# Attention scores and decay sums: the narrow products of one layer are given all 128 rows of the array

## The chip, the core and the metric

The kernel runs on one core of a Trainium2 chip. The metric is the device time of one execution in microseconds (us). A core has a tensor engine (PE) with an array of 128 rows by 128 columns, a vector engine (DVE), a scalar engine (ACT), a GpSimd engine (POOL), a queue engine for transfers (SP), an on-chip memory of 128 partitions and an accumulator memory (PSUM) that the PE writes. For every product the PE first loads a stationary operand (the profile lists that as PEld), then streams the columns of the other operand past it. How many partitions the operands have is how many rows of the array the product uses.

## The reference

One layer on 512 tokens of width 1024: an RMS norm, one projection into three token mixers (gated linear attention, softmax attention, gated DeltaNet), a gated merge of the three, an output projection, then a SwiGLU feed-forward and a last norm. The change touches two small places. In the softmax attention there are 8 heads of 64 channels, and each needs its scores:

```
qh = heads(q) * ATT_HD ** -0.5
scores = jnp.einsum('bhid,bhjd->bhij', q_, k_, preferred_element_type=F32) + bias
p = jax.nn.softmax(jnp.where(valid, scores, -jnp.inf), axis=-1)
```

In the DeltaNet the running sum of a head's log decays is needed along the columns of a score matrix:

```
gc = jnp.cumsum(to_chunks(log_alpha, GDN_HEADS)[..., 0], axis=-1)
gamma = jnp.exp(jnp.where(incl, gc[..., :, None] - gc[..., None, :], -jnp.inf))
```

## The kernel before

Operands are float32, but the large products run on a faster rounded form of it: each operand is split into a high part (rounded) and a low part (what is left), and a product is the sum of high x high, high x low and low x high. `mm3` (L162 to L165) issues these three. A projection (`proj_T`, tile `pj`) is 24 such products of 128 columns by 512 tokens; the value projection (`pv`), the merge (`br`) and the feed-forward (`ff`, `acc`) are of the same kind. They fill the PE from the start to the end.

Between them stand the small steps of the mixers. They are written as generators ("chains"), and `adv` traces as many of their steps behind each large product as a table of estimated delays (`LAT`) says are due. The result is one fixed order of instructions for each engine. An engine executes its own order strictly, and waits where an operand or a buffer is not ready.

**Attention.** `att_proj` prepares a pair of heads; a head has 64 channels, half of the partitions. For head 0 the query tile holds the high parts in partitions 0 to 63 and the low parts in 64 to 127; the key tile `k` has the high parts of the keys on both halves. So one product of 128 rows, L798, gives high x high plus low x high. The third term, query high x key low, is the second product, L799; the low parts of the keys of both heads share one tile `kl`, one head on each half, and the product takes 64 rows:

```
ps = SM("sc")
T.matmul(ps[:, 0:n_], q[hh][:, cs(qb)], k[hh][:, 0:n_], start=True, stop=False)
T.matmul(ps[:, 0:n_], q[hh][rows, cs(qb)], kl[rows, 0:n_], start=False, stop=True)
```

There are 4 pairs, 2 heads in each and 4 blocks of 128 queries, so 32 score tiles `sc`, with 256 to 512 columns. Behind them DVE scales and adds the bias (L801), takes the maximum (L804), ACT the exponential (L805), DVE the reciprocal and the scaling (L806, L807); the PE transposes the result (L813, `pT`), ACT copies it (L815), and the PE multiplies by the values (L822, `ov`; these products use 64 columns of the array).

**Decay sums.** `gcs` holds the high parts of the cumulated decays of the heads in partitions 0 to 7 and the low parts in 32 to 39, zeros between. A product with a selecting matrix `sel` (ones in two rows for a head) adds both and spreads the sum over 128 partitions (tile `rb`, 512 columns, 40 rows). It is done once per head in `gdn_k` (L578) and once in `gdn_q` (L616): 8 products.

Buffers come from pools in rotation. `U` tiles (29 buffers of 128 x 512) serve the queries, keys, convolved DeltaNet inputs (`cvo`) and others. Tiles `w`, `wh`, `wl` are the raw, high and low parts of a weight group (L151 on ACT, L155 on DVE).

Of the kernel before, what the change touches and what calls it, by code (L numbers as in the profile page):

```python
# [7 lines left out]
F32 = mybir.dt.float32  # L8
# [8 lines left out]
P = 128  # L17
S = 512
D = 1024
# [9 lines left out]
HP = 10000  # L29
# order of the projections between the chains  # L30
SEQ = "qyAzv01cdDsLa3rb2"
# [5 lines left out]
XE = "GAVVAAVV"  # L37
# start: 0-3 statistics of a token tile, a-d its norm and transposition, A-D its parts, w x the parts of a
# weight group, m n (M N) its products with the first (second) half of the tokens; engines of the halves of
# the token tiles (XE norm, LE low parts) and of the statistics (SQE), of the weights' parts (WHG, WLG)  # L40
START = "0w1abA2B3xmdcDCnMN"
NWARM = 14
SQE = "VVAV"
LE = "GVGVVVGG"
# estimated delays of the chains' steps, for the order in which they are traced
LAT = dict(ho0=9.069, ho1=0.144, ho2=0.738, ks0=0.985, ks1=0.887, ks2=1.018, gk0=1.523, gk1=3.393, gk2=18.451,
# [9 lines left out]
def trunk(ctx, tc, a, out, dbg=None):  # L56
# [26 lines left out]
    def U(s, dt=F32):  # L83
        return up.tile([P, 512], dt, tag="u", name=nm(s))
# [20 lines left out]
    def h4(t):  # L105
        return t.rearrange("p (h n) -> p h n", n=128)
# [11 lines left out]

# [1 line left out]
    cst = cp.tile([P, 8 * P], F32, name="cst")  # L120
# [25 lines left out]

# [1 line left out]
    def parts(raw, n=1024, eng=None, hi_eng=None):  # L148
# [18 lines left out]
    def preload(after):  # L167
        """The table set with both Exp and Ln, right behind `after`."""
        with tc.high_priority():
            p = A.preload_act_table_set(LNEXP)  # L170
        if after is not None:
            tc.add_manual_dep(p.ins, after.ins.name,
                              mybir.DependencyInfo(mybir.DependencyClass.NoSync, mybir.DependencyReason.DATA),
                              reason="act tables")
# [7 lines left out]
    def rsqrt(y, v):  # L182
        """y = v ** -0.5, one Newton step behind the tables."""
        t = st.tile([P, 16], F32, tag="nw", name=nm("nw"), bufs=4)[:, 0:y.shape[1]]
        A.activation(t, v, AF.Ln)
        A.activation(y, t, AF.Exp, scale=-0.5)
        newton(y, v, t)

# [1 line left out]
    def sq_sum(x, dst, eng=None):  # L190
# [9 lines left out]
    def rms_factor(xs, ss=None, eng=None):  # L200
        """xs: the halves of a token tile."""
        if ss is None:
            ss = rms_rows()
            sq_sum(xs[0], ss[:, 0:1])
        sq_sum(xs[1], ss[:, 1:2], eng)
        y, v, t = ss[:, 1:2], ss[:, 2:3], ss[:, 3:4]
        V.tensor_scalar(v, ss[:, 0:1], ss[:, 1:2], 1.0 / D, op0=ALU.add, op1=ALU.mult)
        A.activation(t, v, AF.Ln, bias=eps)
        A.activation(y, t, AF.Exp, scale=-0.5)
        V.tensor_scalar(v, v, EPS, -0.5, op0=ALU.add, op1=ALU.mult)  # L210
        V.scalar_tensor_tensor(t, y, v, y, op0=ALU.mult, op1=ALU.mult)
        V.scalar_tensor_tensor(y, t, 1.5, y, op0=ALU.add, op1=ALU.mult)
        return y
# [18 lines left out]
    class HT:  # L232
        """Channel-major pair of parts: 8 k-tiles of [128, 512]."""

# [11 lines left out]
    hT = HT("hT")  # L246
    # idle products until the first tokens are there keep the tensor engine's clock up
    if NWARM:
# [10 lines left out]
    def first_A(t, rs):  # L259
        """As norm_A, without the gain."""  # L260
        r = []
# [31 lines left out]
    def bcn(t):  # L293
        """[128, 4] to [128, 4, 128]."""
        return t.unsqueeze(2).to_broadcast([P, 4, P])

    def proj_T(src, raw=None):
        """Columns of a packed weight group, channel-major: [128 columns, 512 tokens] in PSUM."""
        wh, wl = load_w(src) if raw is None else parts(raw)
        ps = BIG("pj")  # L300
        for k in range(KT):
            mm3(ps, wh[:, cs(k)], wl[:, cs(k)], hT.hi(k), hT.lo(k), k == 0, k == KT - 1)
        return ps

    def proj_nat(i, mk):
        """Value projection, natural layout: 4 token tiles of [128 tokens, 512 columns]."""
        outs = [*mk("val"), *mk("val")]
# [23 lines left out]

    # column groups of w_in in the packed order
    GQ, GK, GV, GZ, LR, LK, LQ, AQ, AK, MG = 0, 4, 8, 12, 16, 20, 24, 28, 32, 36

# [1 line left out]
    now = [0.0]  # L336
# [37 lines left out]

# [1 line left out]
    gq, gk, gv = [], [], []  # L376
# [15 lines left out]
    def silu_all(ts, after=()):  # L392
        """In one go: one change of the tables for all."""
        with tc.high_priority(offset=500):
# [31 lines left out]
    for h in range(2):  # L426
        gk.append(conv(ps[h], C_CONV + 4 * (4 + h)))
    # low-rank gate input (three times), a and b of the DeltaNet
    with tc.high_priority(offset=HP):
# [13 lines left out]
    def k_proj(h):  # L443
# [22 lines left out]
    gcs, sel = DD("gcs", F32R)  # L466
    gcs, sel = gcs[0:40], h4(sel[0:40])
    G.memset(gcs.bitcast(F32), 0.0)
    A.copy(gcs[0:8], gc)
    V.tensor_tensor(gcs[32:40], gc, gcs[0:8].bitcast(F32), op=ALU.subtract)  # L470
    G.tensor_tensor(sel, ident[0:40, 0:4].unsqueeze(2).to_broadcast([40, H, P]),
                    ident[0:40, 32:36].unsqueeze(2).to_broadcast([40, H, P]), op=ALU.add)
    k_proj(3)
# [7 lines left out]

    # per-token statistics, natural layout [token, head, chunk]
    def nat(s):
# [13 lines left out]

# [1 line left out]
    def head_out(ps, epsc, gcol, gate, mk, dst, h):  # L499
# [25 lines left out]

    # chunk matrices in DRAM; spaced so that the 32x32 diagonal blocks are evenly spaced too
    BS = 32 * P + 32
# [16 lines left out]

# [1 line left out]
    def fl(t):  # L546
# [83 lines left out]

    # ---- inverses of the unit lower triangular matrices: 32x32 diagonal blocks,
    #      64 of them on partitions, even columns on the lower half, odd ones on the upper ----
    def gdn_inv():
# [68 lines left out]

# [1 line left out]
    Sx = [None] * H  # L704
# [54 lines left out]

# [1 line left out]
    aqk, av, o_att = [None] * 4, [], [None] * 4  # L761
    LO, UP = slice(0, 64), slice(64, P)

    def att_proj(p_):
        """Queries: high parts of a head and, on the other half of the partitions, its low parts;
        keys: the high parts on both halves; low parts of the keys of both heads."""
        q, k, kl = [U("q", F32R) for _ in range(2)], [U("k", F32R) for _ in range(2)], U("kl", F32R)
        ps = proj_T(a["wb"][AK + p_])
        for t, r, o in ((k[0], LO, UP), (k[1], UP, LO)):
            A.copy(t[r], ps[r])  # L770
            V.tensor_tensor(kl[r], ps[r], t[r].bitcast(F32), op=ALU.subtract)
            A.copy(t[o], ps[r])
# [9 lines left out]
    def att_pair(pr_):  # L782
# [7 lines left out]
        for qb in range(NT):  # L790
            nk = P * (qb + 1)
            Ls, PT = [], []
            for hh in range(2):
                rows = slice(64 * hh, 64 * hh + 64)
                q, k, kl = aqk[pr_]
                n_ = max(nk, 256)
                ps = SM("sc")
                T.matmul(ps[:, 0:n_], q[hh][:, cs(qb)], k[hh][:, 0:n_], start=True, stop=False)  # L798
                T.matmul(ps[:, 0:n_], q[hh][rows, cs(qb)], kl[rows, 0:n_], start=False, stop=True)  # L799
                L = TT("L")  # L800
# [32 lines left out]

# [1 line left out]
    lg, lk, lq, lv, rg, o_gla = [], [None] * H, [None] * H, [], [None] * H, [None] * H  # L835
# [24 lines left out]

# [1 line left out]
    def gla_head(h):  # L862
# [90 lines left out]

# [1 line left out]
    GRP = LAT["grp"]  # L955
# [44 lines left out]

# [1 line left out]
    y = [None] * KT  # L1002
# [41 lines left out]

# [1 line left out]
    yh, yl = [], []  # L1046
# [57 lines left out]

# [1 line left out]
    acc = [SM("acc") for _ in range(NT)]  # L1106
# [39 lines left out]
    gb = bc_row(2)  # L1146
    # residual of the first half
    ss = [rms_rows() for _ in range(NT)]
# [30 lines left out]
def pack(i):  # L1179
    """Lays the inputs out for the loads; no arithmetic."""  # L1180
    f = lambda n: np.asarray(i[n])
# [56 lines left out]
    r["wbr"] = np.stack(br)  # L1238
    # gates of the merge in the order of the branches above
    m = r["wb"][36:]  # L1240
# [24 lines left out]
```

## Time and profile before

| | |
|---|---|
| time, 3 runs | 1025.85, 1025.72, 1024.86 us; median 1025.72 |
| span of the profiled execution, first to last instruction | 1025.0 us |
| PE busy | 1005.8 us, 98% |
| DVE, ACT, POOL busy | 529.8, 443.4, 139.3 us |
| granted TensorE clock, mean over the span | 0.982 of full speed |
| products of the 64-row form (L799) | 32, between 169.5 and 414.9 us |
| products of the 40-row form (L578, L616) | 8, between 61.0 and 98.5 us |

The profile lists one execution. Products overlap in the PE: the next one starts while the last columns of the one before are still under way, so the duration of one product is longer than the time that it adds. The time that it adds is read from the chain of waits, which gives for each piece the time from the end of the one before it to its own end. Of the profiled execution only the span is listed; it lies 0.7 us under the median of the runs and 0.1 us over the fastest.

### The profile page before, as it was taken

The numbers are of one execution on the slowest core, as the hardware profiler recorded it, in microseconds if no ns is written. First come the engines' busy times: TensorE is split into PE (matmuls) and PEld (weight loads), VectorE is DVE, ScalarE is ACT, GpSimd is POOL, SyncE is SP. The second block draws the span as 40 slices with busy tenths as digits, with TensorE's granted clock in tenths as the row PEclk, the third lists the DMA queues.
The fourth block names the chain that finished last, engine by engine and source line by source line (L and its number), as shares of the span: only waits on it lengthen the run. The fifth ranks groups of instructions, "written<-read, shape, count | busy, mean of one in ns | idle before, by whom it ended". The sixth has DMA issues, their size and how long they took to land.

```text
span 1025.0 us, 13638 instructions
## 1 busy us (share of the span) xinstructions
PE 1005.8 (98%) x5388; PEld 820.6 (80%) x5388; DVE 529.8 (52%) x924; ACT 443.4 (43%) x715; POOL 139.3 (14%) x153
## 2 busy tenths in 40 slices
PE   6999999999999999999999999999999999999996
PEld 5777887887887877777888878988888888888885
DVE  6688845486456677766543545633333333233324
ACT  5366345254554557564453644432222222223313
POOL 5115120000223312232121220000000000000201
PEclk8999998699999999999999999999999999999998
DMA  6424271011332211122223235133223322332322
GB/s 213 166 82 123 81 207 62 22 42 63 92 103 83 82 63 62 63 83 83 74 91 103 82 103 185 63 103 103 100 85 103 103 92 94 103 101 85 103 95 90
DMA packets 33008, 98.31 MB, mean 96 GB/s; under 512 B 3504, under 2 KB 3776, under 8 KB 32944
## 3 DMA queue, kind: packets, MB, share of 16 engines
q1 hardware_dynamic: 31120, 91.14, 26.9%
q0 software_dynamic: 1824, 6.31, 2.2%
q8 instruction: 42, 0.69, 0.3%
q14 instruction: 22, 0.18, 0.1%
HBM read 91.65 MB, written 5.78 MB: 95 GB/s over the span
## 4 chain that ended last, share of the span: by engine, by line
PE 94%; DVE 3%; ACT 1%; issue 1%; DMA 1%; POOL 0%; SPq 0%; DVEq 0%; ACTq 0%; POOLq 0%
PE pj L163 11%; PE pj L165 10%; PE pj L164 10%; PE ff L165 8%; PE ff L164 8%; PE ff L163 8%; PE acc L164 4%; PE acc L163 4%; PE acc L165 4%; PE br L163 2%; PE br L165 2%; PE br L164 2%; PE ov L822 1%; PE pv L163 1%; PE pv L165 1%; PE pv L164 1%
## 5 line engine op out<-in xcount | busy, mean ns | idle before, releaser
L151 ACT CAST wh<-w 128x1024 fp32r<-128x1024 f32 x150 | 157.9, 1053 | 406.0 <-PE ff L164 163.9
L155 DVE TENSOR_TENSOR wl<-w,wh 128x1024 fp32r<-128x1024 f32 x148 | 193.9, 1310 | 258.9 <-ACT wh L151 256.4
L163 PE MATMUL pj<-hTh,wh 128*128 128x512 f32 x464 | 185.5, 400 | 0.6 <-DVE cvo L384 0.6
L165 PE MATMUL pj<-hTh,wl 128*128 128x512 f32 x464 | 185.0, 399 | 0.0
L164 PE MATMUL pj<-hTl,wh 128*128 128x512 f32 x464 | 184.6, 398 | 0.0
L163 PE MATMUL ff<-h2h,wh 128*128 128x512 f32 (+1 forms) x368 | 139.9, 380 | 0.0
L165 PE MATMUL ff<-h2h,wl 128*128 128x512 f32 (+1 forms) x368 | 139.8, 380 | 0.0
L164 PE MATMUL ff<-h2l,wh 128*128 128x512 f32 (+1 forms) x368 | 139.8, 380 | 0.0
L163 PEld LDWEIGHTS pj<-hTh,wh 128*128 128x128 f32 x464 | 87.8, 189 | 19.9 <-issue 2.2
L165 PEld LDWEIGHTS pj<-hTh,wl 128*128 128x128 f32 x464 | 88.0, 190 | 18.9 <-issue 1.6
L164 PEld LDWEIGHTS pj<-hTl,wh 128*128 128x128 f32 x464 | 88.0, 190 | 18.2 <-issue 1.3
L164 PEld LDWEIGHTS ff<-h2l,wh 128*128 128x128 f32 x368 | 69.2, 188 | 13.2
L163 PEld LDWEIGHTS ff<-h2h,wh 128*128 128x128 f32 x368 | 69.2, 188 | 13.1
L165 PEld LDWEIGHTS ff<-h2h,wl 128*128 128x128 f32 x368 | 69.2, 188 | 13.0
L164 PE MATMUL acc<-wl,hh 128*128 128x512 f32 (+1 forms) x162 | 59.5, 367 | 0.0
L163 PE MATMUL acc<-wh,hh 128*128 128x512 f32 (+1 forms) x162 | 59.2, 366 | 0.0
L1169 POOL TENSOR_TENSOR x<-x,gb 128x512 f32<-128x512 f32 x4 | 6.0, 1540 | 343.6 <-ACT sq L195 343.6
L1129 DVE TENSOR_TENSOR silu<-silu,ff 128x512 f32<-128x512 f32 x22 | 15.1, 688 | 72.2 <-PE ff L165 72.2
L165 PE MATMUL acc<-wh,hh 128*128 128x512 f32 (+1 forms) x126 | 46.0, 365 | 0.0
L163 PE MATMUL br<-oh,wh 128*128 128x512 f32 x96 | 38.2, 398 | 0.0
L165 PE MATMUL br<-oh,wl 128*128 128x512 f32 x96 | 37.7, 392 | 0.0
L1029 POOL TENSOR_TENSOR y<-y,yt 128x512 f32<-128x512 f32 x16 | 22.5, 1406 | 110.6 <-DVE yt L1028 110.6
(319 smaller groups left out, 1602.2 us busy)
## 6 DMA issues: line engine op xcount, KB each, us to landing
w<-in_wb SPq DMA_DIRECT2D x60, 512.0 KB, 3.5
w<-in_wfi SPq DMA_DIRECT2D x44, 512.0 KB, 3.5
w<-in_wfo SPq DMA_DIRECT2D x22, 512.0 KB, 3.5
w<-in_wbr SPq DMA_DIRECT2D x12, 512.0 KB, 3.5
w<-in_wv SPq DMA_DIRECT2D x8, 512.0 KB, 3.6
w<-in_wout SPq DMA_DIRECT2D x8, 512.0 KB, 3.5
x<-in_x SPq DMA_DIRECT2D x4, 512.0 KB, 7.2
toe<-in_toe SPq DMA_DIRECT2D x8, 256.0 KB, 2.9
```

The lines of the kernel that those rows point to most:

```text
L151: A.copy(hi, raw)
L155: (eng or V).tensor_tensor(lo, raw, hi.bitcast(F32), op=ALU.subtract)
L163: T.matmul(ps, lh, rh, start=first, stop=False)
L164: T.matmul(ps, lh, rl, start=False, stop=False)
L165: T.matmul(ps, ll, rh, start=False, stop=last)
L822: T.matmul(po[64 * hh:64 * hh + 64, 0:P], av[kt][:, h * 64:(h + 1) * 64], PT[hh][:, cs(kt)], start=kt == 0, stop=kt == qb, tile_position=( ...
L1029: G.tensor_tensor(y[m], y[m], t, op=ALU.add)
L1129: V.tensor_tensor(s, s, pr[1], op=ALU.mult)
L1169: G.tensor_tensor(xt[0], xt[0], gb[:, 0:512], op=ALU.mult)
```

## The change

The low parts of the keys get a tile for each head of a pair instead of one for both. In it the other half of the partitions is set to zero by POOL, and the second product of the scores takes all 128 partitions: the zeros meet the low parts of the queries and add nothing. `gcs` and `sel` are used at their full 128 partitions too, with zeros beyond row 39. All else in the diff is comments taken out; lines of the changed kernel from L770 on have a number that is 2 or 3 higher.

```diff
     gcs, sel = DD("gcs", F32R)
-    gcs, sel = gcs[0:40], h4(sel[0:40])
+    sel = h4(sel)
     G.memset(gcs.bitcast(F32), 0.0)
...
-    G.tensor_tensor(sel, ident[0:40, 0:4].unsqueeze(2).to_broadcast([40, H, P]),
-                    ident[0:40, 32:36].unsqueeze(2).to_broadcast([40, H, P]), op=ALU.add)
+    G.tensor_tensor(sel, ident[:, 0:4].unsqueeze(2).to_broadcast([P, H, P]),
+                    ident[:, 32:36].unsqueeze(2).to_broadcast([P, H, P]), op=ALU.add)
...
-        q, k, kl = [U("q", F32R) for _ in range(2)], [U("k", F32R) for _ in range(2)], U("kl", F32R)
+        q, k, kl = [[U(s, F32R) for _ in range(2)] for s in ("q", "k", "kl")]
+        for t, o in zip(kl, (UP, LO)):
+            G.memset(t[o].bitcast(F32), 0.0)
         ps = proj_T(a["wb"][AK + p_])
-        for t, r, o in ((k[0], LO, UP), (k[1], UP, LO)):
+        for t, l, r, o in ((k[0], kl[0], LO, UP), (k[1], kl[1], UP, LO)):
             A.copy(t[r], ps[r])
-            V.tensor_tensor(kl[r], ps[r], t[r].bitcast(F32), op=ALU.subtract)
+            V.tensor_tensor(l[r], ps[r], t[r].bitcast(F32), op=ALU.subtract)
             A.copy(t[o], ps[r])
...
-                T.matmul(ps[:, 0:n_], q[hh][rows, cs(qb)], kl[rows, 0:n_], start=False, stop=True)
+                T.matmul(ps[:, 0:n_], q[hh][:, cs(qb)], kl[hh][:, 0:n_], start=False, stop=True)
```

The order of the PE, DVE and SP is the same before and after, instruction by instruction. Eight instructions are new on POOL, and one instruction of ACT stands elsewhere.

POOL, in the order of before, behind the transfers of the DeltaNet's triangular matrices (`TU`) and ahead of the first steps of the gated linear attention (`g`, `kq`); `sc` here is the score tile of that mixer, `toe` a table of biases:

```order
L662 DMA TU_1459<-Td 128x4x128 x2
L866 MEMSET sc_2824 64x4x64
L866 MEMSET sc_3162 64x4x64
L787 MEMSET toe_2176 64x64
L787 MEMSET toe_2179 64x64
```

The same place in the order of after:

```order
L662 DMA TU_1462<-Td 128x4x128 x2
L770 MEMSET kl_1391 64x512
L770 MEMSET kl_1392 64x512
L868 MEMSET sc_2833 64x4x64
L868 MEMSET sc_3174 64x4x64
L770 MEMSET kl_2106 64x512
L770 MEMSET kl_2107 64x512
L790 MEMSET toe_2182 64x64
L790 MEMSET toe_2185 64x64
```

The zeros of the first pair of heads come ahead of the two `sc` instructions, those of the second pair right behind them. The zeros of the third and fourth pair stand further on, among the `kq` steps.

ACT, in the order of before, around the first of the four casts that split the keys of the second pair (tile `k`), in the recurrence of the DeltaNet (`vn` is its product, `cvo` its result):

```order
L815 COPY PT_1749<-pT_1746 128x256
L770 CAST k_2101<-pj_2110 64x512
L815 COPY PT_1754<-pT_1751 128x256
L721 COPY cvo_1288<-vn_1756 128x128
L721 COPY cvo_1330<-vn_1760 128x128
```

In the order of after the cast stands 18 rows later:

```order
L817 COPY PT_1872<-pT_1868 128x384
L817 COPY PT_1878<-pT_1874 128x384
L826 CAST oh_1518<-ov_1892 128x128
L773 CAST k_2104<-pj_2116 64x512
L721 COPY cvo_1248<-vn_1923 128x128
```

With more `U` tiles in rotation, this `k` tile and the two `kl` tiles of the second pair now get the buffers of the convolved keys of the DeltaNet's heads (`cvo`), which the recurrence's products L715 (`kS`) read until its last chunk.

## Rows read from the trace of the kernel before

**Rows 1.** The page: busy time of the engines; engines of the chain that ended last.

```profile
PE 1005.8 (98%) x5388; PEld 820.6 (80%) x5388; DVE 529.8 (52%) x924; ACT 443.4 (43%) x715; POOL 139.3 (14%) x153
...
PE 94%; DVE 3%; ACT 1%; issue 1%; DMA 1%; POOL 0%; SPq 0%; DVEq 0%; ACTq 0%; POOLq 0%
```

**Rows 2.** Busy by stretch: PE, PEld, DVE, ACT, POOL, granted clock, DMA, GB/s.

```profile
75.00:89.00 14.00, 13.38 (x67) 11.01 (x66) 13.85 (x17) 8.09 (x12) 10.58 (x16) 1.00 0.38 112
160.00:215.00 55.00, 54.95 (x465) 43.68 (x464) 29.78 (x84) 21.43 (x61) 0.56 (x2) 0.78 0.09 30
215.00:232.00 17.00, 17.00 (x125) 14.31 (x124) 16.18 (x47) 11.88 (x29) 0.55 (x2) 1.00 0.21 63
```

**Rows 3.** The narrow products by line: duration min/median/max in ns; array rows*columns.

```profile
L578 PE MATMUL rb<-gcs x4: 492/498/498, 61.0 to 69.2; 40*128 40x512 f32 x4
...
L799 PE MATMUL sc<-kl,q x32: 379/438/579, 169.5 to 414.4; 64*128 64x256 f32 x16, 64*128 64x384 f32 x8, 64*128 64x512 f32 x8
```

**Rows 4.** Chain of waits around a decay sum: start us, us that it adds, what.

```profile
61.05 0.42 PE rb L578
61.47 0.43 PE pj L164
61.90 0.23 PE pj L165
```

**Rows 5.** Chain of waits: two score tiles of 256 columns between full products.

```profile
229.63 0.12 PE sc L798
229.75 0.31 PE sc L799
...
230.38 0.31 PE sc L799
230.68 0.43 PE pj L165
```

**Rows 6.** Timeline of the weight loads in that stretch: start us, us, engine, line.

```profile
230.30 0.18 PEld L799 LDWEIGHTS sc<-kl,q 64*128 64x128 f32 x1
...
230.72 0.19 PEld L163 LDWEIGHTS pj<-hTh,wh 128*128 128x128 f32 x1
```

**Rows 7.** Chain of waits at other places: 256 columns, 384 columns, 112 rows.

```profile
991.22 0.12 PE acc L164
...
201.42 0.18 PE sc L798
201.60 0.37 PE sc L799
...
267.29 0.23 PE zg L849
```

**Rows 8.** Chain of waits in the stretch of the low clock.

```profile
187.00 0.51 PE sc L799
...
195.60 0.43 PE pj L164
```

**Rows 9.** Timeline (POOL, ACT), chain (L715) and groups (L639) where orders change.

```profile
211.12 0.56 POOL L866 MEMSET sc<- 64x256 f32 x2 [71.49 <-PE S L725]
...
196.07 0.58 ACT L770 CAST k<-pj 64x512 fp32r<-64x512 f32 x1
...
214.23 0.71 ACT L721 COPY cvo<-vn 128x128 f32<-128x128 f32 x3 [1.89 <-PE vn L720]
...
212.03 0.86 PE kS L715 x6
...
L639 POOL MEMSET X<- 128x512 f32 x1 | 0.5, 517 | 0.0
```

**Rows 10.** Timeline: three places where the PE runs close behind DVE.

```profile
85.25 0.47 PE L163 MATMUL pj<-hTh,wh 128*128 128x512 f32 x1 [0.62 <-DVE cvo L384]
...
363.17 0.28 DVE L807 TENSOR_SCALAR L<-L,mx 128x128 f32<-128x128 f32 x1
...
363.67 0.27 PE L813 MATMUL pT<-cst,L 128*128 128x128 f32 x1
```

More of the change, by code (lines that the diff above doesn't have):

```diff
@@ L793, in att_pair @@
             for hh in range(2):
-                rows = slice(64 * hh, 64 * hh + 64)
                 q, k, kl = aqk[pr_]
```

## Prediction

> **What bounds the kernel now.** I read the page first: the PE is busy for 98% of the span and makes up 94% of the chain that ended last, while DVE and ACT are at half load [rows 1]. Time is therefore won where the PE gets through its fixed order sooner, and lost where it then has to wait for another engine. By stretch the picture is the same where the touched products run, with an exception to come back to: between 215 and 232 us DVE has work for 16.18 of 17 us [rows 2].
>
> Next I looked at what the narrow products cost. Their durations, about 0.44 and 0.50 us, say little, since products overlap [rows 3]. The chain of waits tells what each adds. A full product of 512 columns adds 0.23 us; a decay sum of 512 columns on 40 rows adds 0.42, and so does the full product behind it, 0.43; the one after that is back at 0.23 [rows 4]. The same in the scores: of four products of 256 columns in a row, the first, a full one behind full ones, adds 0.12, the other three 0.31 each (two are shown), and the full product behind them 0.43 instead of 0.23 [rows 5]. It is not the number of columns (256 columns of full form add 0.12 elsewhere), and it is not that rows are missing as such: a product of 112 rows among full ones adds 0.23 [rows 7]. What the dear ones have in common is that the form of the array, full or 64 rows, differs from that of the product before. 40 rows count as the small form, 112 as the full one.
>
> The weight loads show how. L163's load starts at 230.72, 0.39 us before its predecessor's piece ends at 231.11: it is hidden. L799's load starts at 230.30, only 0.08 before its predecessor's piece ends at 230.38 [rows 5, 6]. At a change of form the next load waits until the array is nearly empty, and about 0.19 to 0.20 us that are otherwise hidden come to light, at each change.
>
> The Trainium skill has a rule that would give another result here. "TensorE: Matmul & The Clock Gate", section "Why this matters for your kernels", says that a single product of few rows takes the same time as one of 128, and its Part 3 adds that a weight load overlaps the product in flight only when the row groups differ. By that the 64 rows would cost nothing and the load behind another row group would be the hidden one. The trace shows the opposite of the second sentence, as told; what the first one would make of the time is the first rival below.
>
> **The change part by part.**
>
> *Decay sums.* 8 products, each of which loses two changes of form, one ahead and one behind: (0.42 - 0.23) + (0.43 - 0.23) = 0.39 us [rows 4]. 8 x 0.39 = 3.1 us.
>
> *Second score products, change ahead.* Of the 32, 30 follow the full product L798 directly; the other two follow a product of the values, whose form differs from the full one too, so they keep their change. 28 of the 30 run at the full clock: 0.31 - 0.12 = 0.19 at 256 columns, 0.37 - 0.18 = 0.19 at 384 [rows 5, 7], 0.42 - 0.23 at 512 by the decay sum's row [rows 4]. 28 x 0.19 = 5.3 us. Two run in a stretch of half clock: there 512 full columns add 0.43, so 256 should add 0.21, and the product adds 0.51 [rows 8]: 2 x 0.30 = 0.6 us.
>
> *Second score products, change behind.* Counted along the PE's sequence, 22 of the 32 are followed by a product of the full form: 0.43 - 0.23 = 0.20 each [rows 5], 4.4 us. The other 10 are followed by products of 32, 64 or 64-column forms; there the change of form comes later by one product and costs the same.
>
> Together 3.1 + 5.3 + 0.6 + 4.4 = 13.4 us less work for the PE. Its order is unchanged, and no product is added.
>
> *Zeros on POOL.* 8 instructions of 512 columns, at 0.52 us as for a zeroing of the same width [rows 9]: 4.1 us on an engine that is at 14% [rows 1]. The first pair's come where POOL falls idle, at 139.63 (211.12 less the 71.49 that it waits there), 30 us ahead of the first second product at 169.5 [rows 3, 9]. The second pair's stand behind the two `sc` zeroings, which start at 211.12, and they need buffers that the kS products read, whose run at 212.03 is over by 212.89 [rows 9]; so they end at about 214, and the first score of that pair is at 229.75 [rows 5]. The gap of some 16 us hides them; without it the PE would wait for the difference. The third and fourth pair's stand among the kq steps; at 0.5 us each, on an engine with 86% idle time, I expect no one to wait. I take 0; the bounds are 0 and, if all eight delayed POOL's chain and that the PE, 4.1 us. Wider `gcs` and `sel` have the same columns per partition: 0.
>
> *The moved cast on ACT.* It lands where ACT is idle for 1.89 us, from 212.34 to 214.23, and the kS products that hold its buffer are over by 212.89; with its 0.58 us it ends by 213.5, inside the idle time [rows 9]. I take 0; if the idle time were not there, it would delay the recurrence once by 0.58 us, and before 200 us, where it leaves, it can free as much.
>
> *What is late next.* The PE then arrives earlier at values that other engines make. Most of these shift with it, since they start from PE results themselves; where an engine is dense, they don't. (a) At 85.25 the PE already waits 0.62 us for DVE, which has worked 13.85 of 14 us [rows 2, 10]. DVE's dense run starts from weights that the PE releases behind three of the four first decay sums, so of 1.6 us 1.1 pass through and 0.5 are lost. (b) Between 215 and 232 DVE is full; the two score products just ahead of it and in it (0.39 each) cannot be used: 0.8 lost. (c) Around 363.7 the transposition starts 0.22 us behind the scaling of its scores (363.17 + 0.28 = 363.45) [rows 10], and the PE will be there up to 0.5 us sooner relative to it; over the tight places of the third and fourth pair I take 0.8 lost. (d) In the small-matrix steps around 170 us the PE follows ACT closely; 0.4 lost, and 0.2 for the rest. Sum 2.7 us. The bounds are 0 and about half of the 13.4, if every score saving behind a DVE-made value were lost.
>
> 13.4 - 2.7 = 10.7 us. Against the profiled span of 1025.0 that is 1014.3; the runs' median lies 0.7 higher, 1025.7, so I forecast 1015.0 us for the timed runs.
>
> **Rivals.**
>
> *The rows don't matter.* Then what costs is the score product's place (accumulating into a tile just written, weights that repeat), and with 128 rows it still adds 0.31: 1025.7 us. For it: nothing here runs L799 with full rows. Against it: the decay sums do not accumulate and pay the same, and the full product behind pays too [rows 4, 5]. 4%.
>
> *Absorbed.* The PE gets ahead, but DVE, which sets the pace where scores are made, does not, and half of the gain turns into waits: 1025.7 - 6.7 = 1019 us. For it: [rows 10] and the 16.18 of 17 us. Against it: over 160 to 215 us DVE has work for 29.78 of 55 us [rows 2]. 16%.
>
> *The clock.* In 160 to 215 us the granted clock is 0.78 [rows 2]: (1 - 0.78)/0.5 x 55 = 24 us at 1.2 instead of 2.4 GHz, after a spell of small products. If fewer idle moments around the scores let it rise sooner, up to 12 us more come back; I take 8: 1007 us. Against it: of that spell's work only four narrow products change. 7%. A shift of the low stretch against the work, which now comes about 2.5 us sooner, is worth half of that, 1.3 us either way, and is in the range.
>
> *Slower: POOL's queue.* The zeros of the second pair wait behind the `sc` zeroings and for a buffer. If they came late, the PE would stand at that pair's first score, with all large products queued behind. It turns the sum once they end 10.7 us after 229.75, at 240.5, which is 26 us later than worked out; at 243 us the whole gain is gone and 2.5 us more, 1028 us. Against it: POOL's rows [rows 9]. 3%.
>
> **How the numbers follow.** The forecast has 70%, with a range of its own from 1012 (all 13.4 and a little of the clock) to 1018. Absorbed 16%, clock 7%, no effect 4%, slower 3%. The range for 8 in 10 is 1011 to 1020: it takes in the absorbed case and leaves out the clock at one end, no effect and slower at the other. A measurement of this kernel tells 0.2%, 2 us, from no change. Faster by more than that: 70 + 16 + 7 = 93%; within it 4%; slower 3%.
>
> **What will show it.** In the changed profile the second score products (then L801) should add 0.12, 0.18 and 0.23 us in the chain, the decay sums and their followers 0.23, and the load of the second score product should start well before the first one's end. Changes of form beside `ov` and the small matrices should stay at 0.43. The span up to 100 us should be 2 to 3 us shorter, and all of the rest gained by 425 us; behind that nothing should differ. I am wrong if L801 still adds 0.31, or if the PE shows new waits behind DVE (the scaling of the scores, the convolution) that add up to more than 5 us, or if POOL's zeros are waited for.

## The result, and the profile after

The changed kernel took 1012.59 us (median of 4 runs: 1012.88, 1013.28, 1012.29 and 1004.28), beside 1025.53 us for the kernel before (4 runs). The ratio is 0.986, 95% interval 0.9825 to 0.9895. Run twice more, each time beside the kernel before, it took 1013.25 us (ratio 0.9882, 0.9869 to 0.9894) and 1012.46 us (0.9878, 0.9862 to 0.9893). One of these 12 runs, at 1004.28 us, stands apart; it has a section of its own below. The profiled execution has a span of 1011.2 us, against 1025.0 before: 13.8 us less.

The page after, busy time of the engines and the chain that ended last:

```profile
PE 991.5 (98%) x5388; PEld 816.7 (81%) x5388; DVE 528.1 (52%) x924; ACT 442.8 (44%) x715; POOL 142.6 (14%) x161
...
PE 92%; DVE 3%; ACT 2%; DMA 1%; issue 1%; SPq 0%; POOL 0%; DVEq 0%; ACTq 0%; POOLq 0%
```

Against [rows 1] the PE has the same 5388 products and 14.3 us less work; the 8 new POOL instructions are there (153 to 161, 3.3 us). The kernel is bound as before. The chain of waits in the stretch that answers to [rows 5], two score tiles of 256 columns between full products (start us, us that it adds, what):

```profile
223.32 0.12 PE sc L800
223.44 0.12 PE sc L801
223.56 0.12 PE sc L800
223.68 0.12 PE sc L801
223.80 0.23 PE pj L165
```

Where 0.12, 0.31, 0.31, 0.31 and 0.43 us stood, there are now 0.12 four times and 0.23: 0.77 us less for these two tiles. The weight loads of the same stretch, as in [rows 6] (start us, us, engine, line):

```profile
223.05 0.19 PEld L800 LDWEIGHTS sc<-k,q 128*128 128x128 f32 x1
223.16 0.19 PEld L801 LDWEIGHTS sc<-kl,q 128*128 128x128 f32 x1
...
223.52 0.19 PEld L165 LDWEIGHTS pj<-hTh,wl 128*128 128x128 f32 x1
```

L801's load starts at 223.16, 0.28 us ahead of the end of L800's piece at 223.44; before, it was 0.08 us ahead. The load of the full product behind starts at 223.52, also 0.28 us ahead of 223.80. Loads are hidden again on both sides. The chain around a decay sum, which answers to [rows 4]:

```profile
60.43 0.24 PE rb L578
60.67 0.23 PE pj L164
60.90 0.23 PE pj L165
```

The two groups of [rows 3], by line (duration min/median/max in ns, first and last start):

```profile
L578 PE MATMUL rb<-gcs x4: 389/408/472, 60.3 to 67.5; 128*128 128x512 f32 x4
```

```profile
L801 PE MATMUL sc<-kl,q x32: 277/337/499, 166.3 to 400.9; 128*128 128x256 f32 x16, 128*128 128x384 f32 x8, 128*128 128x512 f32 x8
```

The starts say where the time went. At the first second score product the kernel is 169.5 - 166.3 = 3.2 us ahead, at the last 414.4 - 400.9 = 13.5, and at the end 13.8. So some 3 us come from the decay sums and the start, 10.3 from the stretch of the scores, 0.3 from the last score product and the one behind it, and nothing from what comes later.

The waits of the PE up to 425 us show whether a new one has come in (what waited, for what, us, times, longest):

```profile
PE nT L270 <- DVE xn L267: 2.1, 1, 2.1
PE nT L270 <- POOL xn L267: 1.1, 1, 1.1
PE nT L270 <- ACT xn L265: 1.1, 1, 1.1
PE pj L163 <- DVE cvo L384: 1.0, 1, 1.0
...
PE w L670 <- ACT w1s L672: 0.2, 1, 0.2
```

The same list before, where it differs:

```profile
PE nT L270 <- ACT xn L265: 2.9, 1, 2.9
...
PE nT L270 <- DVE xn L267: 1.1, 1, 1.1
PE nT L270 <- POOL xn L267: 1.0, 1, 1.0
PE pj L163 <- DVE cvo L384: 0.6, 1, 0.6
```

The wait for the convolution at 85 us has grown from 0.6 to 1.0, and 0.2 us are new at 170. The nT waits, for the first tokens, are 5.0 us before and 4.3 after, but the waits of the first projection products behind them (`pj L411`, not shown) are 1.0 us before and 1.7 after: together nothing. They lie ahead of everything the change touches.

POOL's row and ACT's around the second pair of heads, in answer to [rows 9], from the two timelines (idle time before it, and what ended it, in brackets):

```profile
205.21 0.56 POOL L868 MEMSET sc<- 64x256 f32 x2 [66.96 <-PE S L725]
206.66 1.09 POOL L770 MEMSET kl<- 64x512 f32 x2 [0.89 <-PE kS L715]
```

```profile
207.08 0.58 ACT L773 CAST k<-pj 64x512 fp32r<-64x512 f32 x1 [0.59 <-PE kS L715]
207.99 0.71 ACT L721 COPY cvo<-vn 128x128 f32<-128x128 f32 x3 [0.33 <-PE vn L720]
```

The zeros wait for the kS product as forecast and end at 207.75, 15.7 us before their first use at 223.44; the moved cast ends at 207.66, and ACT is idle behind it for 0.33 us. Last, the stretches of [rows 2] (PE, PEld, DVE, ACT, POOL, granted clock; DMA, GB/s). They are the same times on the clock, but the work in them comes up to 7 us sooner, so the line that holds the work of 215 to 232 us before is put beside them:

```profile
75.00:89.00 14.00, 12.99 (x71) 10.87 (x70) 12.94 (x14) 8.45 (x12) 9.88 (x15) 1.00 0.39 119
160.00:215.00 55.00, 54.82 (x498) 45.95 (x498) 32.06 (x89) 24.54 (x68) 1.75 (x5) 0.81 0.12 41
215.00:232.00 17.00, 16.90 (x105) 13.51 (x103) 15.24 (x49) 9.21 (x26) 0.15 (x1) 1.00 0.14 47
...
208.00:225.00 17.00, 16.90 (x130) 14.81 (x129) 16.52 (x47) 12.41 (x32) 0.29 (x2) 1.00 0.19 63
```

### The profile page after: what moved, and what is told of

The parts are those of the page before. It is cut to its first block, busy times and chain, and to the rows that moved or that the text cites. A ratio compares the mean times of both kernels' runs of the same rounds, so it can differ in the third digit from the quotient of the medians.

```text
span 1011.2 us, 13642 instructions
## 1 busy us (share of the span) xinstructions
PE 991.5 (98%) x5388; PEld 816.7 (81%) x5388; DVE 528.1 (52%) x924; ACT 442.8 (44%) x715; POOL 142.6 (14%) x161
## 4 chain that ended last, share of the span: by engine, by line
PE 92%; DVE 3%; ACT 2%; DMA 1%; issue 1%; SPq 0%; POOL 0%; DVEq 0%; ACTq 0%; POOLq 0%
PE pj L163 10%; PE pj L165 10%; PE pj L164 10%; PE ff L164 8%; PE ff L165 8%; PE ff L163 8%; PE acc L164 4%; PE acc L163 4%; PE acc L165 4%; PE br L163 2%; PE br L165 2%; PE br L164 2%; PE ov L824 2%; PE pv L163 1%; PE pv L165 1%; PE pv L164 1%
## 5 line engine op out<-in xcount | busy, mean ns | idle before, releaser
L163 PEld LDWEIGHTS ff<-h2h,wh 128*128 128x128 f32 x368 | 69.2, 188 | 13.2
```

The lines of the kernel that those rows point to most:

```text
L163: T.matmul(ps, lh, rh, start=first, stop=False)
```

## The experiments

The theory: each alternation between the full form of the array (128 rows) and the small one (64) costs 0.19 to 0.20 us, and the change takes 68 of them away (16 at the decay sums, 30 ahead of the second score products and 22 behind them; counted along the PE's sequence there are 191 changes of form before and 123 after). The expectation of the first run says 76; the parts in the two that follow, 52 and 16, make 68. Rivals: the tiles and orders that came with it matter, or the price grows with the rows that a product lacks.

**The changed kernel again**, on the chip of the next three runs, gave 1013.25 us (1012.18 to 1013.65, 4 runs); none of the four lies near 1004. Expected:

> The changed kernel once more, for its spread. Theory (changes of form of the array cost 0.19 to 0.20 us each, and 76 of them went): 12 to 13.5 us under the kernel before, so about 1012 to 1013.5. One of the four runs so far was 1004.3 with a mean clock of 0.994 instead of 0.987. If the stretch of half clock around 180 us comes and goes by chance, some runs again lie near 1004, with a clock of 0.99 or more, and none in between by more than 2 us; if that run was a stray, all lie within 1 us of 1012.6.

**Scores alone.** The decay sums go back to 40 rows:

```diff
-    sel = h4(sel)
+    gcs, sel = gcs[0:40], h4(sel[0:40])
...
```

> Only the second score products take 128 rows; the decay sums keep 40. Theory: the 52 changes of form at the scores go, 10.2 us less PE work, of which 9.5 to 10.2 arrive: 1015.4 to 1016.2. Rival (the gain of 12.9 comes from the lower start of everything or from the clock, not from the forms): the gain stays near 13 or falls by an amount that has nothing to do with 3.1. In the chain a decay sum adds 0.42 us and the product behind it 0.43 again.

Measured: 1015.0 us (1006.91 to 1015.79, 6 runs), ratio 0.9877 (0.9848 to 0.9905). Two runs, 1006.91 and 1007.14, stand apart as one did above; the other four are 1014.99 to 1015.79, median 1015.3, 9.8 us under the 1025.1 us of the kernel before (23 runs beside these four kernels). The chain around a decay sum is that of before:

```profile
60.61 0.42 PE rb L578
61.03 0.43 PE pj L164
61.46 0.23 PE pj L165
```

**Sums alone.** The second score product goes back to one `kl` tile and 64 rows, the decay sums stay at 128:

```diff
...
-                T.matmul(ps[:, 0:n_], q[hh][:, cs(qb)], kl[hh][:, 0:n_], start=False, stop=True)
+                r = slice(64 * hh, 64 * hh + 64)
+                T.matmul(ps[:, 0:n_], q[hh][r, cs(qb)], kl[r, 0:n_], start=False, stop=True)
```

> Only the decay sums take 128 rows; the scores are as before, with 64 rows and one tile of low key parts for both heads. Theory: 16 changes of form go, 3.1 us less PE work, of which 2.5 to 3.1 arrive: 1022.4 to 1023.0. Rival (the waits behind DVE at 84 us take it back): 1025.5. Together with the scores alone it should give the whole change within 1 us.

Measured: 1023.14 us (1022.24 to 1024.29, 11 runs), ratio 0.9979 (0.9971 to 0.9988): 2.0 us, 0.5 less than the least that was expected, though its interval reaches from 1.2 to 3.0. The two parts add up: 9.8 + 2.0 = 11.8 us, beside 1025.1 - 1013.25 = 11.9 for both together.

**All but the rows.** Separate `kl` tiles, zeros, moved cast, order: all as in the changed kernel, but the second product reads only the 64 rows of its head:

```diff
-                T.matmul(ps[:, 0:n_], q[hh][:, cs(qb)], kl[hh][:, 0:n_], start=False, stop=True)
+                r = slice(64 * hh, 64 * hh + 64)
+                T.matmul(ps[:, 0:n_], q[hh][r, cs(qb)], kl[hh][r, 0:n_], start=False, stop=True)
```

> All of the change but one line: low key parts in a tile for each head, with zeros in the other half, and decay sums at 128 rows; the second score product, however, reads only its head's 64 rows. Theory (the form of the product decides): the gain of the scores is gone, the decay sums' stays, so as sums_only: 1022.4 to 1023.0, and in the chain the second products add 0.31 us at 256 columns. Rival (what helps is the separate tiles, since the two heads no longer read one tile, or the moved instructions): 1012 to 1013 as the whole change. Should it be slower than sums_only by up to 1 us, that is the price of the zeros and the moved cast.

Measured: 1022.9 us (1022.2 to 1024.21, 11 runs), ratio 0.9977 (0.9968 to 0.9985), the time of the sums alone. Its chain at the place shown above (the second product is L802 here):

```profile
225.72 0.12 PE sc L800
225.84 0.31 PE sc L802
226.15 0.31 PE sc L800
226.47 0.31 PE sc L802
226.77 0.43 PE pj L165
```

That is [rows 5] to the hundredth, with all the rest of the change in place. The gain hangs on the rows of the product alone, and the zeros and the moved cast cost nothing that 11 runs can tell (1022.9 against 1023.14 us without them).

**72 rows.** Does the form count, or the rows? The decay sums are cut to 72 rows, 56 short of the array:

```diff
-    sel = h4(sel)
+    gcs, sel = gcs[0:72], h4(sel[0:72])
...
```

> The changed kernel, with the decay sums reading 72 rows instead of 128 (the 8 products then lack 56 rows). Theory, only the form of the array counts, and 72 rows already take the full one: the decay sums and the full products behind them add 0.23 us each in the chain of waits, and the time is that of the changed kernel, 1012.6 to 1013.3 us. Rival, a product is dearer the more rows it lacks: with 56 of the 88 rows that were missing before, about 0.12 us more on either side, 0.35 us each in the chain, 8 x 0.25 = 2 us, 1015 us. The theory is wrong if a decay sum adds 0.30 us or more.

Measured: 1012.42 us (1012.21 to 1013.09, 4 runs), ratio 0.9881 (0.9866 to 0.9896), and in the chain:

```profile
60.36 0.23 PE pj L163
60.59 0.23 PE rb L578
60.82 0.23 PE pj L164
```

72 rows cost what 128 cost, 40 rows cost 0.39 us a piece more. It is the form, and missing rows are free within it.

**The runs that stand apart.** Single runs of two kernels were 8 us shorter. Their spans and mean granted clocks: 1002.6 us at 0.994, 1005.2 at 0.996 and 1005.4 at 0.995, while the others have 0.985 to 0.988. If all work took twice as long at half clock, the time lost would be span x (1 - clock): 1002.6 x 0.006 = 6.0 us against 1011.2 x 0.014 = 14.2, and the difference of 8.2 is about what that run is shorter by. These three runs have no profile, so that the clock is their cause is not shown; what could be missing in them is seen in the profiled one, where the granted clock falls to half (1.2 of 2.4 GHz) behind a run of 32x32 products at 171 us, for some 20 us. The next two kernels spread those small products, by the table that sets the order of tracing: with all four level delays doubled, and (shown) at four times their value.

```diff
-... td=6.267, tu=7.889, l0=2.272,
-           l1=2.083, l2=1.091, l3=3.757, ...
+... td=6.267, tu=7.889, l0=9.088,
+           l1=8.332, l2=4.364, l3=15.028, ...
```

> The changed kernel, with the estimated delays of the four levels of the DeltaNet inverse doubled, so that its small products (32x32 and 64x64) are traced among more of the large products. It tests the 8 us that single runs of the changed kernel and of the scores alone were shorter by (1004.3 and 1006.9 beside 1012.9 and 1015.0, at a mean granted clock of 0.994 to 0.996 beside 0.987). Theory, those runs lack the stretch of half clock (171 to 192 us in the profiled run), which sets in behind a run of dense small products: with these spread, the stretch is gone or shorter in every run; half a dozen more changes of form cost 6 x 0.4 = 2.4 us, so 1013 + 2.4 - 8 = 1007 us at a mean clock of 0.994. Rival, the half clock has another cause than the order here: the stretch stays at about 20 us, and the time is 1013 + 2.4 = 1015 us.

Measured: 1006.97, 1007.25, 1012.2 and 1012.8 us (median 1009.73, ratio 0.9854, 0.9826 to 0.9883), clocks 0.997, 0.997, 0.989 and 0.992. Neither forecast holds for all of them: the theory's 1007 us in two runs, one of them the profiled one, where the clock is 1.00 over 170 to 195 us, and in the other two a clock between the extremes.

> As the one before, with the delays of these four levels at four times their value: the small products come in pieces of one to four, over a longer stretch, and stand between large ones nearly everywhere. Theory, the stretch of half clock needs the small products close together: no stretch at 1.2 GHz behind the first 20 us, about ten more changes of form at 0.4 us, 1013 + 4 - 8 = 1009 us. Rival, the order has nothing to do with it: 1017 us, with some 20 us of half clock still there. If the DeltaNet recurrence, which begins later, is waited for at the merge of the branches, up to 10 us come on top; the PE would show idle time there.

Measured: 1008.15 us (1007.77 to 1008.59, 4 runs), ratio 0.9837 (0.9821 to 0.9853), clocks 0.994 to 0.997 in every run. The stretch 170 to 195 us, first of the changed kernel, then with the delays at four times their value:

```profile
170.00:195.00 25.00, 25.00 (x234) 19.91 (x236) 10.71 (x35) 6.49 (x21) 0.00 (x0) 0.59 0.07 22
```

```profile
170.00:195.00 25.00, 24.95 (x291) 18.17 (x291) 15.65 (x42) 11.34 (x31) 1.04 (x2) 1.00 0.15 48
```

The granted clock is 1.00 instead of 0.59. At 0.59 of full speed, (1 - 0.59) x 25 = 10.3 us would be lost here if all work took twice as long; 4.3 us arrive in the time. Matched product by product over the two traces, the products that ran at half clock in the changed kernel add 7.9 us less in the spread one. Some 3 us of that are lost again between 219 and 232 us, where the products of the DeltaNet's recurrence (L715, L720, L725) now run close behind ACT and DVE, with waits that the changed kernel does not have:

```profile
PE vn L720 <- ACT cvo L721: 0.4, 1, 0.4
PE kS L715 <- DVE S L730: 0.2, 1, 0.2
PE kS L715 <- DVE cvo L716: 0.2, 1, 0.2
```

The changes of form are 129 instead of 123, at 0.2 us each about 1 us.

**The spreading without the change** separates the two:

```diff
 (the kernel before, with)
+... l0=9.088, l1=8.332, l2=4.364, l3=15.028 ...
```

> The kernel before, with the delays of the four levels of the DeltaNet inverse at four times their value, as in the last run, and without the change. It tells whether the 4 to 5 us that the spreading gave (1008.2 beside 1012.4 to 1013.3 us) are a matter of their own, or come only with the changed products. Theory, they are their own: the stretch of half clock (173 to 197 us in the kernel before) goes here too, about 8 us less and some 3 us back for the added changes of form, 1020 us; the changed products then account for 1020 - 1008.2 = 12 us, as without the spreading. Rival, the narrow products of the scores are part of what brings the clock down: the stretch stays, and with the added changes of form the time is 1027 us.

> The changed kernel once more, on the same chip as the run beside it: 1012.5 to 1013.5 us, with a single run near 1005 possible. If the spreading is a matter of its own, its worth without the change (1025 less the run beside this) agrees within 1 us with its worth on top of the change (this run's median less 1008.2).

Measured side by side: 1020.24 us (1017.55 to 1021.33, 5 runs), ratio 0.9952 (0.9938 to 0.9966), and 1012.46 us for the changed kernel. In the profiled execution, the fastest of the five, the kernel before has its clock back as well:

```profile
170.00:195.00 25.00, 24.95 (x281) 17.46 (x281) 14.38 (x44) 10.74 (x31) 0.00 (x0) 1.00 0.13 44
```

Its mean clock is 0.997 there and 0.989 to 0.994 in the other four, at 1019.4 to 1021.33 us, so the stretch of half clock is not shown to be gone in them.

By medians the spreading is worth 1024.67 - 1020.24 = 4.4 us without the change and 1012.46 - 1008.15 = 4.3 on top of it; the change is worth 12.2 us without the spreading and 1020.24 - 1008.15 = 12.1 with it. So the gain of the spreading does not hang on the change. How exactly the two add up is less sure than these medians look, since the executions differ in their clock: the two profiled ones, both at 0.997, are 1017.55 - 1008.59 = 9.0 us apart, and the 3 us that the recurrence loses between 219 and 232 us are lost in the one with the change and not in the other. The kernel with both beats both kernels of this study.

## Why the prediction was right, and which term was off

*The mechanism* was as told, and the runs show it: 0.31 to 0.12 at 256 columns, 0.43 to 0.23 for the product behind, 0.42 to 0.24 for the decay sums, at the places named. The price hangs on the alternation between 64 and 128 rows (all but the rows: gain of the scores gone; 72 rows: gain of the sums kept). The first rival, that rows don't matter, is out by the changed kernel's chain and the run with all but the rows.

The prediction weighed a rule of the Trainium skill by which the load behind another row group would be the hidden one; the loads above are hidden only since the form is the same. Another page of the Trainium skill, "TensorEngine Tiling (Array Packing)", section "Key Properties", says that changing the tiling mode, and not merely the tile, drains TensorE. The trace agrees: behind a change the load starts 0.08 us ahead of the end of the piece before, without one 0.28. The section gives no figure; here it is 0.19 to 0.20 us at the full clock for each change.

*The sum, term by term.* The PE's order is the same before and after, so the two traces can be matched product by product: what a product adds is its end less the end of the one before it. Before less after, in us:

| part | forecast | traces |
|---|---|---|
| decay sums and the products behind them | 3.1 | 2.9 |
| second score products | 5.3 + 0.6 | 5.4 + 0.6 |
| the 22 full products behind them | 4.4 | 4.3 |
| *work, together* | 13.4 | 13.2 |
| other products, 60 to 100 us: wait (a) | -0.5 | -0.4 |
| other products, 200 to 425 us: waits (b) and (c) | -1.6 | -0.6 |
| other products up to 60 us | 0 | +0.6 |
| other products around the stretch of half clock: wait (d) and the rest | -0.6 | +1.0 |

The rows add up to 13.8 us, the difference of the two spans. The work is as forecast to 0.2 us. In the timed runs the decay sums alone gave 2.0 us, of the 2.9 - 0.4 = 2.5 that the traces show, and the scores alone, leaving out the two runs that stand apart, 9.8.

*Zeros and moved cast*: 0 forecast for each, and the run with both but without the rows shows nothing. The rival of the POOL queue is out: the margin was 15.7 us, where some 16 were forecast.

*What is late next* is the term that was mis-sized: 2.7 us forecast, 1.0 seen. Wait (a) came as told, 0.4 us more behind the convolution. Waits (b) and (c), 0.8 us each, came to some 0.4 and 0.2, too short for the PE's list of waits, which has nothing between 200 and 425 us. The reason I gave for (b), DVE at 16.18 of 17 us, read a busy share as a limit: with the same work some 7 us earlier DVE is as full (16.52 of 17 us over 208 to 225), and the PE's list shows no wait for it. The largest of these delays, 0.3 us, stands behind a copy of ACT ahead of a transposition, in the chain after (first two lines) and before (last):

```profile
216.97 0.48 ACT PT L817
...
217.50 0.66 PE pT L815 x4
...
224.03 0.46 PE pT L813 x4
```

At the place of (d), around 170 us, about 0.1 us was lost. The absorbed rival is out with them.

*The rest of this one pair* goes with the clock. The first 0.6 us lie ahead of the first decay sum (61.05 against 60.43), where the waits sum to the same and the granted clock over the first 60 us is 0.94 before and 0.97 after. The 1.0 us comes with a stretch of half clock that was shorter by some 3 us in this execution. Nothing shows it to come from the change: in the trace of the changed kernel run again the stretch is as long as before, and with the sums alone it is as short as after (0.71). From 165 to 200 us, before, after and again:

```profile
165.00:200.00 35.00, 34.95 (x327) 26.67 (x327) 15.19 (x43) 11.86 (x36) 0.00 (x0) 0.66 0.09 31
165.00:200.00 35.00, 34.82 (x348) 28.14 (x348) 16.84 (x54) 10.95 (x37) 0.00 (x0) 0.71 0.10 32
165.00:200.00 35.00, 34.85 (x332) 27.93 (x333) 15.55 (x52) 10.41 (x35) 0.00 (x0) 0.66 0.09 32
```

There the touched products and those behind them give 13.2 us again, and 0.9 us are lost at the places of (a), (b) and (c). By the traces the change itself is then worth 13.2 - 1.0 = 12.2 us, and the medians of the two later comparisons, 11.9 and 12.2 us, say the same. The forecast of 10.7 was too low by the waits that did not come. The size of the work was no luck, since each of its terms came out by itself.

*The clock* as a rival had the right size (8 us less) and was given 7%; the place is not shown, since no run that was so much shorter has a trace. By the mean clock it came true in 1 of 12 runs of the changed kernel and 2 of 6 with the scores alone. The 72-row kernel's 4 runs, 43 runs of the kernel before and 22 with narrow scores did not show it. Three of 22 with wide scores against none of 65 without hints that the wide scores help; it is too few to build on, and what decides it from run to run stays open.

## What to carry to other kernels

Read the price of a narrow product from the chain of waits, ahead of it and behind it, and not from its duration: where it stands alone between full ones, filling its operand with zeros up to the next form is free work for the array and saves both changes of form, here 0.39 us each time; where the next product has another form anyway, as behind 10 of the 32 here, only the change ahead of it is saved. A busy engine beside the bound is no wait yet; ask first whether its work starts from the results that come earlier. And a stretch of lowered clock behind small products is worth its own experiment, since the order alone may bring the clock back.

## What was not expected of the hardware

72 rows behave as 128 (0.23 us) and 40 as 64 (0.42). The stretch of half clock depends on how the small products stand in the order: with them as traced, 0.59 of full speed in 170 to 195 us; spread at four times the delays, 1.00 in the profiled execution, with and without the change. The mean clock tells of the others: 0.994 to 0.997 in all four runs with the change, but 0.989 to 0.994 in four of five without it; at double the delays, two runs at 0.997 and two at 0.989 to 0.992 of the same program, 5 us apart.
